# Down projection: two products' activations stored as high and low parts, read back ready-made, and seven weight tiles instead of four

## The chip, the cores and the metric

The kernel runs on one core of one Trainium2 chip, as one program. The metric is the device time of that program in microseconds. A core has five engines that run their own instruction streams and meet only at semaphores: TensorE (PE, matrix products), VectorE (DVE), ScalarE (ACT), GpSimd (POOL) and SyncE (SP, which here issues most DMA transfers). An instruction that waits for a semaphore holds up everything behind it on its own engine; this holds for the DMA issues on SP too.

## The reference, cut to what matters

One encoder layer on 1024 tokens of width 1024: a modulated norm, one input projection, attention and mLSTM heads, an output projection, then the feed-forward part and a final norm. The change lies in the feed-forward part, whose hidden width is 2816:

```python
h = modulate(rms_norm(x, norm_ffn_g[l]), sh2, sc2)
ffn = (jax.nn.silu(h @ w_gate[l]) * (h @ w_up[l])) @ w_down[l]
x = x + g2[:, None, :] * ffn
return rms_norm(x, final_norm_g)
```

All inputs and outputs are float32.

## The kernel before, in words

**High and low parts.** A float32 matrix product is made of three TensorE products of rounded operands (`mm3`, L311 to L314): each operand x is split into a high part (a copy into the type fp32r, made by ACT) and a low part (x minus the high part, made by DVE or POOL), and high·high, high·low and low·high are added up in one PSUM bank. For the activations of the down projection these parts are the tiles `whi` and `wlo` (six buffers each, from the pool `wp`), for its weights `wch` and `wcl`.

**The gate and up stage.** The 2816 hidden columns are 22 tiles of 128; two of them are a pair, p = 0 to 10. For each pair the kernel forms the gate and up products by a seven-product scheme (Strassen's kind, over halves of the width and halves of the tokens), and then, in `act_sums` (L1632), the left operands that the down projection's own seven products need: sums and differences of four blocks of the activation. `store_act` writes them to device memory as the tensors `act_d[p][m]`, 128x512 each, by DMAs on ACT's queue.

**The down projection.** `DOWN` names its seven products in the order in which they run: 11, 21, T2, T3, T1, 22, T4. A product sums over the eleven pairs. One pair of one product, called a step below, is twelve 128x512 matmuls: four output tiles times the three of `mm3`. (T4 runs as two halves of 128x256.) In `down` (L1732) a step first waits for its activation parts and its weight parts, then runs, and then calls three things for what comes later:

- `load_piece`, which asks for the activation of the sixth step ahead. Before, this is a load from `act_d` into one of three tiles `wst` on SP's queue (issued up to two pieces earlier still), then a split by ACT (`whi`) and POOL (`wlo`; on DVE in T4's second half);
- `load_w`, which makes the next weight parts from weight rows that lie in SBUF: ACT copies `wch`, DVE subtracts `wcl`, four buffers each. For T2 DVE first makes two differences (a11 - a21 and `s`), and one more behind `wcl`: four DVE operations for a pair;
- `load_rows`, which issues the pending loads in the list `todo` on SP's queue: the weight rows `wd` of `w_down` (512 KB each, 22 of them) and the tiles `x` of the residual. It goes on while the planner's estimate of the DMA backlog is below 4 us, and issues at least one.

**Names of weight rows.** In the instruction lists `wd` is followed by c (0 or 1: which tile of the pair) and p: `wd10` is c = 1, p = 0, `wd010` is c = 0, p = 10. Product 11 uses rows with c = 0, product 21 rows with c = 1, T2 both. The first five pairs of product 11 take their weights by another way (a 256 KB load, split like an activation), because the weight rows can only be loaded when the pools of the gate and up stage are closed. That happens in `open_down` (L1660), once all stores of activations (`stored`) are done.

**What sets the order.** The kernel is written as Python generators and chains that run against a planner's clock (`Clock`), and the instructions are emitted in the order in which that clock reaches them. A tile asked for from a pool takes over the buffer of the oldest tile of its name; the instruction that writes it waits until the last reader of the old one is done.

Of the kernel before, what the change touches and what calls it, by code (L numbers as in the profile page):

```python
# [11 lines left out]
F32 = mybir.dt.float32  # L12
F32R = mybir.dt.float32r
BF16 = mybir.dt.bfloat16
AF = mybir.ActivationFunctionType
# [5 lines left out]
P = 128  # L21
S = 1024
D = 1024
KT = D // P
HALF = 512
# [18 lines left out]
KB = 5  # L44
AHEAD = 2
NP = NF // 2
# [3 lines left out]
FF = [("b", p) for p in range(NB)] + [("v", 0)] + [("s", (p, i)) for p in range(1, NP - 1) for i in range(2)] + [("v", NP - 1)]  # L50
SET = ["A11", "A12", "S2", "S3", "S1", "A22", "S4"]
DOWN = ["11", "21", "T2", "T3", "T1", "22", "T4"]

# [196 lines left out]
def layer_kernel(ctx, tc, xT, c, w_ada, vecs, cons, rope, w_f, w_fT, w_t0, w_t, w_o, w_gu, w_d, out):  # L250
# [42 lines left out]
    ya_d = [dram.tile([P, S], F32, name=f"ya_d{i}") for i in range(4)]  # L293
    x1_d = [dram.tile([P, S], F32, name=f"x1_d{i}") for i in range(KT)]
    act_d = [{m: dram.tile([P, HALF], F32, name=f"act_d{p}{m}") for m in DOWN} for p in range(NP)]

# [68 lines left out]
    with tc.manual_schedule():  # L365
# [44 lines left out]
        def pair_w(p):  # L410
            order = ("A11", "A12", "S2", "S3", "S4", "S1", "A22") if p else ("S4", "S2", "S3", "S1", "A22")
            return [("set", (p, i, m)) for m in order for i in range(2)]

        def down_w():
            out = []
            for m in DOWN:
                for c in range(2 if m == "T4" else 1):
                    for p in range(NP):
                        a = act_d[p][m]
                        a = a[:, 256 * c:256 * (c + 1)] if m == "T4" else a  # L420
                        n = 2 if m == "T4" else 4
                        out.append((a.rearrange("p (a b) -> p a b", a=n), n, P, c))
                        if m == "11" and p < KB:
                            out.append((w_d[2 * p][:, 0:HALF].rearrange("p (a b) -> p a b", a=4), 4, P))
            return out
# [62 lines left out]
        def load_piece():  # L488

            i = len(pieces)  # L490
            if i == len(specs):
                return
            while len(made) <= min(i + (AHEAD if i + AHEAD >= start["down"] else 0), len(specs) - 1):
                piece(len(made))
            p, there, st = made[i]
            pieces.append(p)
            if isinstance(specs[i][0], str):
                set_piece(p, *specs[i][1])
                return
            split(p, 0.0, lambda: st[0], [P, *specs[i][1:3]], there,  # L500
                  lo=dve if specs[i][3:] == (1,) or i < 9 or start["m", 2] <= i < start["b", 1] else None)
# [1130 lines left out]
        def act_sums(p):  # L1632
            S, T = SG[p], {}
            stored.append(Flag())
            end = stored[-1]
            for m in ("22", "21"):
                ck.chain(0.0, a_ok[p, m], lambda m=m: store_act(p, m, S[m]))

            def new(m, a, b):
                T[m] = fp.tile([P, HALF], F32, tag="tt", name="tt", bufs=4)  # L1640
                dve.tensor_sub(T[m], a, b)

            ck.chain(0.0, a_ok[p, "12"], a_ok[p, "22"], lambda: new("T3", S["22"], S["12"]),
                     lambda: store_act(p, "T3", T["T3"]), a_ok[p, "11"],
                     lambda: dve.tensor_sub(S["12"], S["12"], S["11"]), lambda: store_act(p, "T1", S["12"]),
                     lambda: new("T2", S["22"], S["12"]), lambda: store_act(p, "T2", T["T2"]), a_ok[p, "21"],
                     lambda: new("T4", S["21"], T["T2"]), lambda: store_act(p, "T4", T["T4"]), flag=end)

# [5 lines left out]
        x1_ok = {(k, n): Flag() for k in range(KT) for n in range(NH)}  # L1654
        wseq = [(m, c, p) for m in DOWN for c in range(2 if m == "T4" else 1) for p in range(NP)
                if m != "11" or p >= KB]
# [3 lines left out]
        def open_down():  # L1660
# [16 lines left out]
            load_rows()  # L1677
            for _ in range(4):
                load_w()
# [9 lines left out]
        def load_w():  # L1689
# [32 lines left out]
            def hi():  # L1722
                e[0] = pb.tile([P, HALF], F32R, tag="wch", name="wch", bufs=4)
                act.activation(e[0], src, AF.Copy)

            def lo():
                e[1] = pb.tile([P, HALF], F32R, tag="wcl", name="wcl", bufs=4)
                eng.tensor_sub(e[1], src, e[0].bitcast(F32))
# [3 lines left out]
        def down():  # L1732
            i = start["down"]
            flat = lambda t: t.rearrange("p a b -> p (a b)")
            for m in DOWN:
                for c in range(2 if m == "T4" else 1):
                    w = 256 if m == "T4" else HALF
                    banks = []
                    for p in range(NP):
                        t = pieces[i]  # L1740
# [5 lines left out]
                        for o in range(4):  # L1746
                            if p == 0:
                                yield [slot("acc")]
                                banks.append(psum_tile([P, w], "acc"))
                            mm3(banks[o][0], [x[:, o * P:(o + 1) * P] for x in wt], [flat(x) for x in t[:2]],  # L1750
                                p == 0, p == NP - 1)
                            ck.pe(0.65 * w / HALF)
# [3 lines left out]
                        if opened3.done and not early:  # L1756
                            load_w()
                        if m == "22" and p < 4:
                            load_w()
# [557 lines left out]
```

## Time and profile before

| | us |
|---|---|
| median of 3 runs | 1377.88 |
| lowest and highest run | 1376.33, 1381.36 |
| time of the profiled execution | 1373.45 |
| span of the profiled execution (first to last instruction) | 1371.6 |
| PE busy in the span | 1279.8 (93%) |
| DVE, ACT, POOL busy | 1043.1, 708.9, 697.2 |

All times are microseconds from the span's start. The profiled execution took 1373.45 us, of which 1.85 us lie around its span, and is 4.4 us shorter than the median. The gate and up stage ends and the down projection's first matmul starts at 1130.52; the first 128x256 matmul (T4) starts at 1325.48.

### The profile page before, as it was taken

The numbers are of one execution on the slowest core, as the hardware profiler recorded it, in microseconds if no ns is written. First come the engines' busy times: TensorE is split into PE (matmuls) and PEld (weight loads), VectorE is DVE, ScalarE is ACT, GpSimd is POOL, SyncE is SP. The second block draws the span as 40 slices with busy tenths as digits, with TensorE's granted clock in tenths as the row PEclk, the third lists the DMA queues.
The fourth block names the chain that finished last, engine by engine and source line by source line (L and its number), as shares of the span: only waits on it lengthen the run. The fifth ranks groups of instructions, "written<-read, shape, count | busy, mean of one in ns | idle before, by whom it ended". The sixth has DMA issues, their size and how long they took to land.

```text
span 1371.6 us, 19596 instructions
## 1 busy us (share of the span) xinstructions
PE 1279.8 (93%) x6596; PEld 1074.1 (78%) x6596; DVE 1043.1 (76%) x1541; ACT 708.9 (52%) x1344; POOL 697.2 (51%) x580
## 2 busy tenths in 40 slices
PE   7889888899999979999999999999999999979997
PEld 5777677788778878877778788888888887857887
DVE  6937698975789748768698989877766654998876
ACT  6576366688577755454477522333333234344462
POOL 0353577655558436687605155545454455545542
PEclk9999999999999999999999999999999999989999
DMA  9444433233233146562553344332233159623324
GB/s 360 158 134 142 122 90 96 75 97 109 66 113 99 61 133 195 186 235 100 192 191 116 101 145 151 126 107 101 102 113 116 62 186 349 255 78 107 100 59 157
DMA packets 105044, 188.07 MB, mean 137 GB/s; under 512 B 11632, under 2 KB 33264, under 8 KB 104944
## 3 DMA queue, kind: packets, MB, share of 16 engines
q1 hardware_dynamic: 91552, 164.73, 37.6%
q10 hardware_dynamic: 13392, 22.10, 4.2%
q8 instruction: 52, 0.85, 0.3%
q14 instruction: 48, 0.39, 0.1%
HBM read 139.86 MB, written 43.25 MB: 133 GB/s over the span
## 4 chain that ended last, share of the span: by engine, by line
PE 55%; DVE 20%; issue 8%; ACT 6%; POOL 5%; DMA 4%; SPq 1%; DVEq 0%; ACTq 0%; POOLq 0%
PE acc L314 14%; PE acc L312 14%; PE acc L313 14%; DVE sst L98 3%; DVE y L98 3%; DVE x L98 2%; PE av L1210 2%; DVE PT L98 2%; PE T L1191 2%; PE S L1159 2%; POOL wlo L98 1%; DVE wd L98 1%; DVE s L98 1%; DVE Cs L98 1%; PE ni L1997 1%
## 5 line engine op out<-in xcount | busy, mean ns | idle before, releaser
L98 POOL TENSOR_TENSOR wlo<-wst,whi 128x512 fp32r<-128x512 f32 (+2 forms) x191 | 272.2, 1431 | 293.3 <-ACT whi L98 239.9
L98 ACT ACTIVATE whi<-wst 128x512 fp32r<-128x512 f32 (+2 forms) x223 | 133.1, 605 | 114.2 <-PE acc L314 27.6
L313 PE MATMUL acc<-x,whi 128*128 128x512 f32 x352 | 136.9, 389 | 0.0
L98 POOL TENSOR_SCALAR P<-P,sst 128x1024 f32<-128x1024 f32 x64 | 86.8, 1357 | 87.8 <-DVE sst L98 66.9
L98 POOL TENSOR_TENSOR wlo<-wr,whi 128x512 fp32r<-128x512 f32 x52 | 72.2, 1389 | 71.5 <-ACT whi L98 68.5
L312 PE MATMUL acc<-hh,whi 128*128 128x512 f32 x224 | 97.1, 433 | 7.7 <-ACT xp L98 6.2
L312 PE MATMUL acc<-whi,wch 128*128 128x512 f32 x244 | 96.8, 397 | 5.4 <-ACT wch L98 5.4
L314 PE MATMUL acc<-whi,wcl 128*128 128x512 f32 x244 | 96.8, 397 | 2.9 <-DVE wcl L98 2.8
L313 PE MATMUL acc<-wlo,wch 128*128 128x512 f32 x244 | 96.4, 395 | 0.2 <-POOL wlo L98 0.2
L98 ACT ACTIVATE P<-S,sst,colq 128x1024 f32<-128x1024 f32 x64 | 77.2, 1206 | 35.1 <-DVE sst L98 28.8
L98 DVE TENSOR_TENSOR PT<-T,PT 128x512 fp32r<-128x512 f32 x128 | 83.4, 681 | 9.3 <-ACT PT L98 9.1
L313 PE MATMUL acc<-hl,whi 128*128 128x512 f32 x224 | 90.0, 402 | 0.0
L314 PE MATMUL acc<-hh,wlo 128*128 128x512 f32 x224 | 89.8, 401 | 0.0
L98 ACT ACTIVATE whi<-wr 128x512 fp32r<-128x512 f32 x56 | 35.4, 632 | 100.2 <-DVE wr L98 49.1
L98 ACT ACTIVATE PT<-T 128x512 fp32r<-128x512 f32 x128 | 71.8, 596 | 28.6 <-PE T L1191 27.9
L1191 PE MATMUL T<-ident,P 128*128 128x128 f32 x512 | 72.2, 279 | 15.3 <-DVE PT L98 10.4
L312 PE MATMUL acct<-whi,hh 128*128 128x256 f32 (+1 forms) x256 | 81.6, 319 | 4.9 <-ACT hh L98 3.6
L98 DVE TENSOR_REDUCE sst<-S 128x1 f32<-128x1024 f32 x64 | 77.7, 1214 | 10.4 <-PE S L1159 8.9
L98 POOL TENSOR_TENSOR wlo<-s,whi 128x512 fp32r<-128x512 f32 x40 | 55.1, 1377 | 49.1 <-ACT whi L98 49.1
L1191 PEld LDWEIGHTS T<-ident,P 128*128 128x128 f32 x512 | 59.2, 143 | 25.9 <-issue 9.8
L98 POOL TENSOR_TENSOR ada<-ada,cond 128x512 f32<-128x512 f32 x48 | 68.1, 1419 | 21.9 <-DMA ada<-in_w_ada_dram 21.4
L98 DVE TENSOR_TENSOR wcl<-wd,wch 128x512 fp32r<-128x512 f32 x50 | 51.4, 1041 | 35.7 <-ACT wch L98 35.5
(486 smaller groups left out, 3853.9 us busy)
## 6 DMA issues: line engine op xcount, KB each, us to landing
wr<-in_w_gu_dram SPq DMA_DIRECT2D x66, 256.0 KB, 2.7
ada<-in_w_ada_dram SPq DMA_DIRECT2D x64, 256.0 KB, 3.3
wd<-in_w_d_dram SPq DMA_DIRECT2D x22, 512.0 KB, 6.4
wst<-in_w_gu_dram SPq DMA_DIRECT2D x42, 256.0 KB, 3.0
wst<-act_d SPq DMA_DIRECT2D x33, 256.0 KB, 4.2
ada<-in_w_ada_dram SPq DMA_DIRECT2D x16, 512.0 KB, 7.3
wst<-in_w_o_dram SPq DMA_DIRECT2D x32, 256.0 KB, 3.8
act_d<-sg ACTq DMA_DIRECT2D x29, 256.0 KB, 2.1
```

Of the source, the lines that this page charges most:

```text
L98: return fn(*args, **kw)
L312: nc.tensor.matmul(acc, w[0], x[0], start=first, stop=False)
L313: nc.tensor.matmul(acc, w[0], x[1], start=False, stop=False)
L314: nc.tensor.matmul(acc, w[1], x[0], start=False, stop=last)
L1159: nc.tensor.matmul(sp[:, halves(n)], qs[:, j * P:(j + 1) * P], k2[g][m][:, halves(n)], start=m == 0, stop=m == 1)
L1191: nc.tensor.transpose(tp[:, k], Pt[q][:, (4 * b + k) * P:(4 * b + k + 1) * P], ident)
L1210: nc.tensor.matmul(av, va[:, k, h // 4], PT[it][m][:, k], start=(k, m) == (0, 0), stop=(k, m) == (NJ - 1, 1))
L1997: nc.tensor.matmul(ni, x["q"][:, i * P:(i + 1) * P], H["Cs"][b][:, i4], start=True, stop=True)
```

## The change

Three things are changed.

1. For products 21 and T2 (`PARTS`), `act_sums` no longer stores the activation itself. At the end of a pair's chain it makes the high part on ACT (a new tile `th`, one buffer) and the low part on DVE (in place), and stores both as `part_d[p][m, 0]` and `[m, 1]`, by two DMAs instead of one. In the down projection `load_piece` loads these two straight into `whi` and `wlo`; the split by ACT and POOL goes for those 22 steps.
2. The order of pairs in a product (`turn`) is 0 to 10 for products 11 and 21, as before, and 5 to 10 and then 0 to 4 for the other five.
3. `wch` and `wcl` have seven buffers instead of four, and `open_down` asks for seven weight tiles ahead.

```diff
+PARTS = ("21", "T2")
...
+        def turn(m):
+            return [*range(NP)] if m in ("11", "21") else [*range(KB, NP), *range(KB)]
+
         def down_w():
             out = []
             for m in DOWN:
                 for c in range(2 if m == "T4" else 1):
-                    for p in range(NP):
+                    for p in turn(m):
+                        if m in PARTS:
+                            out.append(("parts", (p, m)))
+                            continue
...
+            if specs[i][0] == "parts":
+                q, m = specs[i][1]
+                for x, tag in enumerate(("whi", "wlo")):
+                    p[x] = lined(tag, [P, 4, P])
+                    arrive = dma(p[x].rearrange("p a b -> p (a b)").bitcast(F32), part_d[q][m, x])
+                ck.chain(arrive, lambda: None, flag=p[2])
+                return
...
-            for m in ("22", "21"):
-                ck.chain(0.0, a_ok[p, m], lambda m=m: store_act(p, m, S[m]))
+            ck.chain(0.0, a_ok[p, "22"], lambda: store_act(p, "22", S["22"]))
...
+            def parts(m, t):
+
+                def hi():
+                    T[m, 0] = fp.tile([P, HALF], F32R, tag="th", name="th", bufs=1)
+                    act.activation(T[m, 0], t(), AF.Copy)
+
+                def lo():
+                    dve.tensor_sub(t().bitcast(F32R), t(), T[m, 0].bitcast(F32))
+
+                def store():
+                    for i, x in enumerate((T[m, 0].bitcast(F32), t())):
+                        f = Flag()
+                        stored.append(f)
+                        ck.chain(dma(part_d[p][m, i], x, nc.scalar), lambda: None, flag=f)
+
+                return hi, lo, store
...
-                     lambda: new("T2", S["22"], S["12"]), lambda: store_act(p, "T2", T["T2"]), a_ok[p, "21"],
-                     lambda: new("T4", S["21"], T["T2"]), lambda: store_act(p, "T4", T["T4"]), flag=end)
+                     lambda: new("T2", S["22"], S["12"]), a_ok[p, "21"],
+                     lambda: new("T4", S["21"], T["T2"]), lambda: store_act(p, "T4", T["T4"]),
+                     *parts("21", lambda: S["21"]), *parts("T2", lambda: T["T2"]), flag=end)
...
-            for _ in range(4):
+            for _ in range(7):
                 load_w()
...
-                e[0] = pb.tile([P, HALF], F32R, tag="wch", name="wch", bufs=4)
+                e[0] = pb.tile([P, HALF], F32R, tag="wch", name="wch", bufs=7)
...
-                    for p in range(NP):
+                    for at, p in enumerate(turn(m)):
```

How the instructions move is shown at two places. The first is SP's queue where the weight rows of product 21 are loaded. Before, these are the rows from the last activation of product 11 (`act_d1011`) on; `act_d021` is product 21's activation of pair 0, and each load into `wst` waits for POOL, which empties that tile.

```order
L317 DMA wst_11393<-act_d1011_184 128x512 [waits DMAHW1_49,Pool_49]
L317 DMA wst_11407<-act_d021_115 128x512 [waits DMAHW2_49,Pool_49]
L317 DMA wd10_11269<-in_w_d_dram 128x1024 [waits DMAHW3_49]
L317 DMA wd11_11270<-in_w_d_dram 128x1024 [waits DMAHW4_49]
L317 DMA wst_11424<-act_d121_122 128x512 [waits DMAHW5_49,Pool_49]
L317 DMA wd12_11271<-in_w_d_dram 128x1024 [waits DMAHW6_49]
L317 DMA wd13_11272<-in_w_d_dram 128x1024 [waits DMAHW7_49]
L317 DMA wd14_11273<-in_w_d_dram 128x1024 [waits DMAHW0_49]
L317 DMA wst_11460<-act_d221_129 128x512 [waits DMAHW1_49,Pool_49]
```

The same place on SP's queue now; `part_d5210` is the high part of product 21's pair 5, `part_d5211` its low part, and so on.

```order
L320 DMA whi_11611<-part_d5210_134 128x512 [waits DMAHW2_49,PE_49,Pool_49]
L320 DMA wlo_11613<-part_d5211_135 128x512 [waits DMAHW3_49]
L320 DMA wd10_11427<-in_w_d_dram 128x1024 [waits DMAHW4_49]
L320 DMA whi_11652<-part_d6210_138 128x512 [waits DMAHW5_49,PE_49]
L320 DMA wlo_11654<-part_d6211_139 128x512 [waits DMAHW6_49]
L320 DMA wd11_11428<-in_w_d_dram 128x1024 [waits DMAHW7_49]
L320 DMA whi_11673<-part_d7210_142 128x512 [waits DMAHW0_49,PE_49]
L320 DMA wlo_11675<-part_d7211_143 128x512 [waits DMAHW1_49]
L320 DMA wd12_11429<-in_w_d_dram 128x1024 [waits DMAHW2_49]
L320 DMA whi_11694<-part_d8210_146 128x512 [waits DMAHW3_49,PE_49]
```

The weight rows of product 21 stood between activations of its own first pairs, two or three at a time; now each of them stands alone behind a load of parts that is five pairs ahead of it (`wd10` behind the parts of pair 5), and that load waits for PE, which reads the old contents of the same `whi` buffer. By the six buffers, the parts of pair 5 of product 21 replace product 11's activation of pair 10, those of pair 6 replace product 21's pair 0, those of pair 7 its pair 1, and so on: in the built program the semaphore value of each such wait is that of the last matmul of that step.

The second place is ACT's queue at the end of the gate and up stage, for the last pair. Before, `act_d10T2`, `act_d1021` and `act_d10T4` are the stores of that pair's T2, 21 and T4.

```order
L317 DMA act_d10T2_186<-tt_11196 128x512 [waits DMAHW5_49,DVE_49]
L317 DMA act_d1021_185<-sg_11020 128x512 [waits DVE_49]
L98 ACTIVATE whi_11218<-wst_11161 128x512 [waits DMAHW1_49,PE_49,Pool_49]
L317 DMA act_d10T4_190<-tt_11212 128x512 [waits DMAHW0_49,DVE_49]
L98 ACTIVATE whi_11231<-wst_11188 128x512 [waits DMAHW2_49,PE_49]
L98 ACTIVATE whi_11254<-wst_11221 128x512 [waits DMAHW6_49,PE_49,Pool_49]
```

The same place on ACT's queue now:

```order
L99 ACTIVATE whi_11340<-wst_11285 128x512 [waits DMAHW5_49,PE_49,Pool_49]
L320 DMA act_d10T4_234<-tt_11335 128x512 [waits DMAHW2_49,DVE_49]
L99 ACTIVATE th_11343<-sg_11144 128x512
L99 ACTIVATE whi_11356<-wst_11312 128x512 [waits DMAHW6_49,PE_49]
L320 DMA part_d10210_154<-th_11343 128x512 [waits DMAHW4_49,Activation_49]
L320 DMA part_d10211_155<-sg_11144 128x512 [waits DVE_49]
L99 ACTIVATE th_11365<-tt_11320 128x512 [waits DMAHW4_49]
L320 DMA part_d10T20_156<-th_11365 128x512 [waits DMAHW7_49,Activation_49]
L320 DMA part_d10T21_157<-tt_11320 128x512 [waits DMAHW0_49,DVE_49]
L99 ACTIVATE whi_11386<-wst_11345 128x512 [waits DMAHW1_49,PE_49,Pool_49]
```

The stores of 21 and T2 moved from ahead of T4's store to behind it. The second `th` takes the one buffer of the first, and so waits, on ACT, until the first high part has been stored; the splits `whi` for product 11 stand behind it. On TensorE the order of the twelve matmuls of each step is unchanged. On POOL the run of `wlo` splits in the down projection has 49 rows instead of 71.

More of the change, by code (lines that the diff above doesn't have):

```diff
@@ L294, in layer_kernel @@
     x1_d = [dram.tile([P, S], F32, name=f"x1_d{i}") for i in range(KT)]
+    part_d = [{(m, i): dram.tile([P, HALF], F32, name=f"part_d{p}{m}{i}") for m in PARTS for i in range(2)}
+              for p in range(NP)]
     act_d = [{m: dram.tile([P, HALF], F32, name=f"act_d{p}{m}") for m in DOWN} for p in range(NP)]
@@ L1654, in layer_kernel @@
         x1_ok = {(k, n): Flag() for k in range(KT) for n in range(NH)}
-        wseq = [(m, c, p) for m in DOWN for c in range(2 if m == "T4" else 1) for p in range(NP)
+        wseq = [(m, c, p) for m in DOWN for c in range(2 if m == "T4" else 1) for p in turn(m)
                 if m != "11" or p >= KB]
@@ L1722, in hi @@
             def hi():
-                e[0] = pb.tile([P, HALF], F32R, tag="wch", name="wch", bufs=4)
+                e[0] = pb.tile([P, HALF], F32R, tag="wch", name="wch", bufs=7)
                 act.activation(e[0], src, AF.Copy)
             def lo():
-                e[1] = pb.tile([P, HALF], F32R, tag="wcl", name="wcl", bufs=4)
+                e[1] = pb.tile([P, HALF], F32R, tag="wcl", name="wcl", bufs=7)
                 eng.tensor_sub(e[1], src, e[0].bitcast(F32))
@@ L1746, in down @@
                         for o in range(4):
-                            if p == 0:
+                            if at == 0:
                                 yield [slot("acc")]
@@ L1750, in down @@
                             mm3(banks[o][0], [x[:, o * P:(o + 1) * P] for x in wt], [flat(x) for x in t[:2]],
-                                p == 0, p == NP - 1)
+                                at == 0, at == NP - 1)
                             ck.pe(0.65 * w / HALF)
@@ L1757, in down @@
                             load_w()
-                        if m == "22" and p < 4:
+                        if m == "22" and at < 4:
                             load_w()
```

## The prediction

> **What bounds the kernel now.** The page's head says that TensorE is busy 93% of the span. I then read the busy times by stretch, to see where the rest is (columns: stretch, its length, busy time of PE, PEld, DVE, ACT and POOL with instruction counts, granted TensorE clock, DMA share, GB/s).
>
> ```profile
> PE 1279.8 (93%) x6596; PEld 1074.1 (78%) x6596; DVE 1043.1 (76%) x1541; ACT 708.9 (52%) x1344; POOL 697.2 (51%) x580
> ...
> 1090.00:1130.00 40.00, 40.00 (x178) 33.15 (x177) 23.50 (x29) 12.60 (x21) 20.09 (x15) 1.00 0.52 172
> 1160.00:1190.00 30.00, 30.00 (x135) 24.82 (x133) 27.55 (x32) 12.92 (x22) 15.75 (x12) 1.00 0.89 342
> 1200.00:1220.00 20.00, 12.90 (x41) 9.52 (x41) 19.90 (x24) 9.36 (x18) 8.90 (x6) 0.74 0.32 93
> 1220.00:1240.00 20.00, 19.06 (x82) 14.80 (x81) 18.93 (x19) 9.30 (x17) 11.52 (x8) 1.00 0.32 83
> ```
>
> In the gate and up stage (first stretch) PE never stops. In product 21 (second) it doesn't either, with DMA at 0.89. It stops in product T2 (third): 7.1 us idle, DVE busy 19.90 of 20, and the clock at 0.74. The waits of PE over the six full-width products (us in total, times, longest) name what ended them:
>
> ```profile
> PE acc L312 <- ACT wch L98: 5.4, 3, 4.7
> PE acc L314 <- DVE wcl L98: 2.8, 2, 2.4
> PE acc L314 <- POOL wlo L98: 0.5, 1, 0.5
> PE acc L313 <- POOL wlo L98: 0.2, 1, 0.2
> ```
>
> So it is T2's weight parts, not its activations, that PE waits for. The timeline of PE gives the sizes (start, duration, idle time before in brackets):
>
> ```profile
> 1130.52 0.39 PE L312 MATMUL acc<-whi 128*128 128x512 f32 x1
> ...
> 1205.59 0.80 PE L312 MATMUL acc<-whi,wch 128*128 128x512 f32 x1 [4.67 <-ACT wch L98]
> ...
> 1209.24 0.80 PE L314 MATMUL acc<-whi,wcl 128*128 128x512 f32 x1 [2.43 <-DVE wcl L98]
> ...
> 1210.26 0.63 PE L313 MATMUL acc<-wlo,wch 128*128 128x512 f32 x1
> 1210.69 0.63 PE L314 MATMUL acc<-whi,wcl 128*128 128x512 f32 x1
> ...
> 1216.09 0.39 PE L313 MATMUL acc<-wlo,wch 128*128 128x512 f32 x1
> 1216.31 0.39 PE L314 MATMUL acc<-whi,wcl 128*128 128x512 f32 x1
> ...
> 1325.48 0.28 PE L312 MATMUL acc<-whi,a 128*128 128x256 f32 x1
> ```
>
> At full clock matmuls start 0.227 us apart, so a step of twelve takes 2.72. The six products are 792 matmuls, 179.5 us at that pitch; from 1130.52 to 1325.48 they took 195.0. Of the 15.4 lost, about 1 lies in product 11 (the two POOL waits and the restart behind them) and 14 around T2. After the wait of 4.67 the pitch is 0.43: half the clock. When it fell and when it came back, by half microseconds (PE busy, clock, DMA share, GB/s):
>
> ```profile
> 1205.00:1205.50 0.50, 0.00 (x0) 0.67 0.00 0
> 1215.00:1215.50 0.50, 0.50 (x3) 0.59 0.68 143
> ```
>
> It fell some 4.3 us after PE had stopped (at 1200.9), and came back some 6 us after the unbroken run from 1209.24 began.
>
> **The change, part by part.** *What it removes.* Why T2's weights are late, from the costliest groups of DVE and POOL between 1188 and 1236 (times, then busy us and mean ns of one):
>
> ```profile
> L98 DVE TENSOR_TENSOR s<-wd,wd 128x512 f32<-128x512 f32 x10 | 12.8, 1280 | 0.0
> L98 DVE TENSOR_TENSOR wd<-wd,s 128x512 f32<-128x512 f32 x11 | 10.7, 983 | 0.0
> L98 DVE TENSOR_TENSOR wd<-wd 128x512 f32<-128x512 f32 x10 | 10.1, 1014 | 0.0
> L98 DVE TENSOR_TENSOR wcl<-s,wch 128x512 fp32r<-128x512 f32 x10 | 9.0, 903 | 2.0 <-ACT wch L98 2.0
> ...
> L98 POOL TENSOR_TENSOR wlo<-wst,whi 128x512 fp32r<-128x512 f32 x17 | 25.1, 1489 | 26.5 <-ACT whi L98 26.5
> ```
>
> Four DVE operations for a pair are 1.28 + 0.98 + 1.01 + 0.90 = 4.2 us, more than a step of 2.72. The change takes the 22 POOL splits and the 22 ACT splits out of 21 and T2, starts T2 with the pairs whose rows come first, and lets DVE run seven tiles ahead. I take the whole 14 us as saved (bounds 8 to 14: the last five pairs of T2 get their first rows only while T2 runs, though needed six steps later).
>
> *Gate and up stage.* For a pair there are two more ACT copies, two more DVE subtractions, two more DMAs on ACT's queue, and ACT waits there until the first `th` is stored (2 to 3 us). I cost it at nothing: in the first stretch above ACT is idle 27 of 40 us and DVE 16, and PE takes its weights from six buffers. If DVE came late to a PSUM bank, PE would show it: bounds 0 to +3.
>
> *The end of that stage.* Here it is on the path, since the weight rows wait for the last store. The chain before: DVE's T4 sum, its store on ACT's queue, the first `wd` on SP's, `wch`, `wcl`, and the first matmul that needs them; behind it the usual landing time of a store (us from issue):
>
> ```profile
> 1133.99 1.67 DVE L98 TENSOR_TENSOR tt<-sg,tt 128x512 f32<-128x512 f32 x1
> ...
> 1135.69 0.33 ACTq L317 DMA_DIRECT2D act_d10T<-tt  x1
> ...
> 1138.92 0.81 SPq L317 DMA_DIRECT2D wd<-in_w_d_dram  x2
> ...
> 1143.45 0.63 ACT L98 ACTIVATE wch<-wd 128x512 fp32r<-128x512 f32 x1 [1.24 <-DMA wd<-in_w_d_dram]
> ...
> 1144.17 0.69 DVE L98 TENSOR_TENSOR wcl<-wd,wch 128x512 fp32r<-128x512 f32 x1 [8.51 <-ACT wch L98]
> ...
> 1144.97 0.39 PE L312 MATMUL acc<-whi,wch 128*128 128x512 f32 x1
> ...
> act_d<-sg ACTq DMA_DIRECT2D x29, 256.0 KB, 2.1
> ```
>
> There is no slack: `wcl` was ready at 1144.86. Now behind T4's store stand on ACT `th` (0.63), a `whi` (0.63), the store of the first `th`, which the second `th` waits for (2.1), that copy (0.63), DVE's subtraction (0.69) and its store: the last store is issued at about 1135.7 + 0.3 + 1.3 + 2.1 + 0.6 + 0.7 = 1140.7 instead of 1135.7. The weight rows, and product 11 from its sixth pair on, come 5 us later. The splits of the fifth pair stand behind the same wait and come late by less. Bounds +3 to +9 (stores of 3 us; rows of the last pairs that now wait for steps 7 and 8).
>
> *Product 21.* This decides. By the order of SP's queue, `wd10`, without which 21 can't begin, stands behind the parts of pair 5, and these wait until the last step of product 11 has read its `whi`. `wd11`, for pair 1, stands behind parts that wait for 21's own first step, and so on: each of the eleven steps begins with a load that was issued only when the step ahead of it had ended. Before, the rows went out well ahead (the first pair of them at 1152.69, some 9 us before product 11 ended), and seven weight tiles don't help, as the rows aren't there. The prices of the link:
>
> ```profile
> 1152.69 1.24 SPq L317 DMA_DIRECT2D wd<-in_w_d_dram  x2
> 1163.14 1.37 SPq L317 DMA_DIRECT2D wd<-in_w_d_dram  x3
> ...
> wd<-in_w_d_dram SPq DMA_DIRECT2D x22, 512.0 KB, 6.4
> ...
> wst<-act_d SPq DMA_DIRECT2D x1, 256.0 KB, 4.2
> ...
> DMA to landing us min/median/max: 3.5/3.8/4.4
> ```
>
> Three issues in 1.37 us are 0.47 apart, so `wd` goes out 0.95 after the parts. How long it takes behind 512 KB of parts on an otherwise empty queue no row shows. The last row is for the three 512 KB loads of `wagain` alone (3.5 at the least); 6.4 is `wd`'s median while the queues are full; 4.2 is a 256 KB load (at 1109.14) behind four others issued within 2.4 us. The last is the nearest case, and I take 4.2 (bounds 3.5 and 6.4). Then come 0.63 for `wch` and some 0.2 (an estimate, from the 0.1 between `wch` and `wcl` and as much at PE and SP) for the meetings: PE is idle 0.95 + 4.2 + 0.63 + 0.2 = 6.0 us a step (bounds 5.3 and 8.2).
>
> The step itself: at full clock its third matmul waits for `wcl` (0.69 behind `wch`), and it lasts 0.75 + 9 x 0.227 + 0.39 = 3.2 us; at half clock 11 x 0.427 + 0.63 = 5.3. A gap of 6.0 is longer than the 4.3 after which the clock fell, and 5.3 of work is shorter than the 6 after which it came back, so most steps run at half clock. Cycle: 9.2 to 11.3, I take 11.0. Against 2.72 that is 8.3 more, eleven times: +91 us (bounds 11 x (5.3 + 3.2 - 2.72) = +64 and 11 x (8.2 + 5.3 - 2.72) = +119).
>
> The Trainium skill, "TensorE: Matmul & The Clock Gate", Part 1, has the clock judged by free-running windows of about 3.4 us: half after a window without work, full after one window of work. This trace's fall after 4.3 us agrees; its return after 6 us is at the far end of what such windows allow. By the page a step of 5.3 us would often contain a whole busy window and end at full clock, which gives back at most some 0.8 us a step, by an estimate from the page: +82 instead of +91.
>
> *T2 and after.* All rows that T2's first six pairs need have landed in 21, and DVE has had ten microseconds a step for its four operations. Its first steps may run at half clock: +2. The later products keep their code; 0.
>
> *Sum.* +5 + 91 + 2 - 14 = +84 on the profiled execution's 1373.45 us: 1457. The three runs have their median 4.4 us above that execution, so I put the forecast at 1460.
>
> **The rivals.** *A lead of one step.* If the wait ahead of `wd` ended a step sooner than I read it, the idle time would be 6.0 - 2.72 = 3.3 us a step, too short for the clock to fall: 11 x 3.6 = +40, less 14, plus 5, so 1409. For it: PE's queue runs ahead in loading weights. Against it: the load overwrites `whi`, which the last matmul of the step reads.
>
> *The rows are in time (the other side).* If the part loads did not hold up the rows behind them, by three steps or more (8.2 us, above the 6.0 of the link), 21 would run through, only the opening would cost 5, and T2's 14 would be saved: 1377.9 + 5 - 14 = 1369. For it: SP's waits cost PE nothing in 21 before, with DMA at 0.89. Against it: those were waits for POOL with the rows ahead of them.
>
> *Only the first row is late.* If later rows caught up while PE waits, the price would be one link, 6 us: 1377.9 + 5 + 6 - 14 = 1375. Against it: one row stands behind each load of parts, eleven times; none can pass.
>
> **How the numbers follow.** The chain of eleven late rows: 0.88. A lead of one step: 0.05. Rows in time: 0.04. One late row: 0.03. The range, from 1433 (opening 3, 64 a product, less 12) to 1486 (nearer the middle than the upper bound of 119, which needs the full queue's landing time on an idle one), leaves some of both ends out with the rivals. A measurement of this kernel can tell about 0.5%, 7 us, from no change: slower 0.93, same 0.03, faster 0.04.
>
> **What would show it.** In the changed kernel's trace: eleven gaps of PE of about 6 us in product 21, ended by ACT's `wch` with `wd` in flight; issues on SP in threes, each just behind the end of a step; the clock near 0.5 to 0.7 in 21; 21 longer than 100 us; no long wait in T2; the first `wd` issued near 1144. I am wrong if `wd` lands in much under 4 us, if the clock holds, or if SP issues rows while a step runs.

## The result, and the profile after

The changed kernel takes 1468.45 us (median of four runs, 1466.09 to 1474.66); the kernel before took 1377.57 beside it (four runs). The ratio is 1.066, with a 95% interval of 1.062 to 1.069. The profiled execution of the changed kernel took 1466.09 us, with a span of 1464.3: 92.7 more than the span before.

The page's head, and behind it the busy times by stretch, with the columns of the table of stretches before:

```profile
PE 1305.3 (89%) x6596; PEld 1087.6 (74%) x6596; DVE 1035.1 (71%) x1563; ACT 708.0 (48%) x1344; POOL 671.3 (46%) x558
```

```profile
1090.00:1130.00 40.00, 40.00 (x179) 33.11 (x178) 23.52 (x31) 13.65 (x23) 20.18 (x15) 1.00 0.55 183
1130.00:1170.00 40.00, 35.13 (x136) 26.25 (x134) 12.52 (x17) 12.08 (x20) 15.22 (x12) 0.91 0.78 266
...
1200.00:1220.00 20.00, 9.68 (x24) 6.96 (x24) 1.39 (x2) 1.26 (x2) 0.00 (x0) 0.67 0.24 81
...
1300.00:1340.00 40.00, 40.00 (x178) 33.13 (x177) 31.42 (x44) 16.62 (x29) 15.16 (x10) 1.00 0.62 205
```

The gate and up stage (first row) still keeps PE busy without a gap, and T2 (last row) now does so too. In product 21 (third row) everything is idle at once: PE half of the time, DVE and ACT nearly always, POOL always, DMA at 0.24. Where no resource is busy, time goes into a chain of latencies. The waits of PE from 1130 to 1430 (us in total, times, longest) say which engine hands over last:

```profile
PE acc L315 <- ACT wch L99: 71.3, 13, 6.9
PE acc L315 <- ACT whi L99: 2.9, 1, 2.9
...
```

One link of that chain, by the timelines of PE, SP and ACT (start, duration, idle time before):

```profile
1200.93 0.79 PE L315 MATMUL acc<-whi,wch 128*128 128x512 f32 x1 [5.43 <-ACT wch L99]
...
1205.69 0.40 PE L317 MATMUL acc<-whi,wcl 128*128 128x512 f32 x1
1212.54 0.79 PE L315 MATMUL acc<-whi,wch 128*128 128x512 f32 x1 [6.45 <-ACT wch L99]
```

```profile
1206.12 0.32 SPq L320 DMA_DIRECT2D whi<-part_d  x1
1206.48 0.43 SPq L320 DMA_DIRECT2D wlo<-part_d  x1
1206.96 0.43 SPq L320 DMA_DIRECT2D wd<-in_w_d_dram  x1
```

```profile
1211.86 0.63 ACT L99 ACTIVATE wch<-wd 128x512 fp32r<-128x512 f32 x1 [10.98 <-DMA wd<-in_w_d_dram]
```

The step's last matmul ends at 1206.09. SP, which had stood waiting for it, issues the parts 0.03 us later and the weight row 0.87 after that end; 4.90 us later the row is there and ACT starts; 0.68 later the next step starts. There are eleven such gaps, ten of them 5.4 to 6.5 us long and the first 6.95. From 1177.17 to 1291.82 there are ten cycles, 11.47 us each.

The lengths of the products show where the 92.7 us are (first matmul of a product to that of the next; product 21 of the changed kernel from the end of product 11's last step, at 1170.2):

| us | 11 | 21 | T2 | T3 | first matmul to T4 |
|---|---|---|---|---|---|
| before | 31.4 | 29.9 | 42.8 | 31.0 | 195.0 |
| after | 39.5 | 126.9 | 30.3 | 29.9 | 286.5 |

Product 21 costs 97.0 more, the opening 8.1 more; T2 gives 12.5 back and T3 1.1.

### The profile page after: what moved, and what is told of

Its sections match the earlier page's. It is cut to its first block, busy times and chain, and to the rows that moved or that the text cites. A ratio compares the mean times of both kernels' runs of the same rounds, so it can differ in the third digit from the quotient of the medians.

```text
span 1464.3 us, 19615 instructions
## 1 busy us (share of the span) xinstructions
PE 1305.3 (89%) x6596; PEld 1087.6 (74%) x6596; DVE 1035.1 (71%) x1563; ACT 708.0 (48%) x1344; POOL 671.3 (46%) x558
## 4 chain that ended last, share of the span: by engine, by line
PE 55%; DVE 17%; DMA 9%; issue 8%; ACT 5%; POOL 4%; SPq 2%; ACTq 0%; DVEq 0%; POOLq 0%
PE acc L315 15%; PE acc L317 14%; PE acc L316 14%; DMA wd<-in_w_d_dram 4%; DVE sst L99 3%; DVE x L99 2%; DVE y L99 2%; DVE PT L99 2%; PE av L1226 2%; PE T L1207 2%; SPq L320 2%; PE S L1175 1%; POOL wlo L99 1%; DVE Cs L99 1%; PE acct L317 1%
## 5 line engine op out<-in xcount | busy, mean ns | idle before, releaser
L99 POOL TENSOR_TENSOR wlo<-wst,whi 128x512 fp32r<-128x512 f32 (+2 forms) x169 | 241.3, 1434 | 423.4 <-ACT whi L99 404.3
L99 ACT ACTIVATE whi<-wst 128x512 fp32r<-128x512 f32 (+2 forms) x201 | 120.0, 603 | 122.4 <-POOL wlo L99 29.1
L315 PE MATMUL acc<-whi,wch 128*128 128x512 f32 x244 | 107.0, 438 | 71.3 <-ACT wch L99 71.3
L99 DVE TENSOR_TENSOR wcl<-wd,wch 128x512 fp32r<-128x512 f32 x50 | 47.6, 956 | 127.5 <-ACT wch L99 127.3
L315 PEld LDWEIGHTS acc<-whi,wch 128*128 128x128 f32 x244 | 51.3, 210 | 87.8 <-ACT wch L99 78.2
L317 PE MATMUL acc<-whi,wcl 128*128 128x512 f32 x244 | 103.7, 425 | 0.7 <-DVE wcl L99 0.7
L316 PE MATMUL acc<-wlo,wch 128*128 128x512 f32 x244 | 103.7, 425 | 0.0
L99 ACT ACTIVATE wch<-wd 128x512 fp32r<-128x512 f32 x50 | 31.2, 624 | 124.3 <-DMA wd<-in_w_d_dram 114.1
L1207 PE MATMUL T<-ident,P 128*128 128x128 f32 x512 | 70.7, 275 | 16.5 <-DVE PT L99 11.4
```

Source lines behind the costliest of these rows:

```text
L99: return fn(*args, **kw)
L315: nc.tensor.matmul(acc, w[0], x[0], start=first, stop=False)
L316: nc.tensor.matmul(acc, w[0], x[1], start=False, stop=False)
L317: nc.tensor.matmul(acc, w[1], x[0], start=False, stop=last)
L1207: nc.tensor.transpose(tp[:, k], Pt[q][:, (4 * b + k) * P:(4 * b + k + 1) * P], ident)
```

## The experiments

**The theories.** A: each step of 21 waits for a weight row that stands in SP's queue behind loads of parts, which wait for the end of the step ahead; its place in the queue is the cause. B: the doubled bytes of the activations are the cause, wherever the rows stand. Besides, it was open how much the half clock costs, what the opening's loss hangs on, and which part of the change saves T2's time. Each kernel was timed beside the kernel before on the same chip; that kernel's median there is given. Single profiled executions begin the down projection anywhere from 1127.9 to 1137.5 us, also where two kernels differ only behind that point, so stages are compared by their lengths and kernels by their medians. The lengths of stages are those of one execution each; where it lay far from its kernel's median, the text says so.

### 1. The rows of 21 one step further ahead

```diff
-        def load_rows():
+        def load_rows(most=99):
...
-            while todo and (ck.dma_t - ck.now < 4.0 or n == 0):
+            while todo and (ck.dma_t - ck.now < 4.0 or n == 0) and n < most:
...
+                        if m == "21":
+                            load_rows(1)
                         load_piece()
...
-                        load_rows()
+                        if m != "21":
+                            load_rows()
```

> Theory A (each weight row of product 21 is issued on SP only when the step before has ended): here the same rows are issued one step earlier, one row a step from the second on. The first row still costs 6.9 us, then two steps pass for one link of 6.4 idle plus 3.2 of work, a cycle near 4.8 instead of 11.5, and the clock is mostly full: product 21 about 60 us instead of 127, total 1402 (1392 to 1415). Rival B (the doubled bytes of the activations make DMA the limit in 21, whatever the order): unchanged within 10 us, 1460 to 1475.

Measured: 1414.05 us beside 1376.21, 1.028 (1.026 to 1.030). Three of PE's waits by its timeline:

```profile
1193.61 0.50 PE L315 MATMUL acc<-whi,wch 128*128 128x512 f32 x1 [2.84 <-ACT wch L99]
1204.84 0.52 PE L315 MATMUL acc<-whi,wch 128*128 128x512 f32 x1 [3.60 <-ACT wch L99]
1215.97 0.80 PE L315 MATMUL acc<-whi,wch 128*128 128x512 f32 x1 [3.69 <-ACT wch L99]
```

The stretch around the second of them, with the clock in the third column from the end:

```profile
1200.00:1210.00 10.00, 6.39 (x21) 4.57 (x20) 2.59 (x4) 1.26 (x2) 0.00 (x0) 0.83 0.54 200
```

With the same bytes, one place in the queue takes some 52 us off (1.066 to 1.028 of 1376), so B falls. PE now waits at every second step only, and two steps go through one turn of the loop of 11.2 us (1193.61 to 1204.84 to 1215.97). A had 9.6 for it, and so 1402: the gaps of about 3 us, which it took to be too short for the clock to fall, still bring it to a mean of 0.83.

### 2. PE kept busy for part of the gap

```diff
+                            for _ in range(16):
+                                nc.tensor.matmul(spare, a[0][:, 0:P], a[1], start=True, stop=True)
```

> Each step of product 21 is followed by sixteen more matmuls into a PSUM bank that nobody reads (3.6 us at full clock), so that TensorE works for a part of each gap; the loads wait for the same matmuls as before. If theory A has the sizes right, idle plus these matmuls is the same 6.4 us a step, the clock stays full and a step of work lasts 3.2 instead of about 5: 11 x 1.9 = 20 us less, 1448 (1442 to 1456). If the half clock is not what lengthens the steps (rival C): 1468, or more by what the added matmuls cost.

Measured: 1463.76 us beside 1376.21, 1.065 (1.062 to 1.069). A miss: nothing like the 20 us came back. The profiled execution took 1475.86 us, the longest of the four (the others 1461.45 to 1465.08). A gap that is left in it, and the clock around it by half microseconds:

```profile
1195.18 2.68 PE L1791 MATMUL acc<-wcl,wch 128*128 128x512 f32 x11
1200.02 0.50 PE L315 MATMUL acc<-whi,wch 128*128 128x512 f32 x1 [2.16 <-ACT wch L99]
```

```profile
1201.00:1201.50 0.50, 0.50 (x3) 0.41 (x3) 0.00 (x0) 0.00 (x0) 0.00 (x0) 1.00 0.00 0
1201.50:1202.00 0.50, 0.50 (x3) 0.36 (x3) 0.00 (x0) 0.00 (x0) 0.00 (x0) 0.61 0.00 0
...
1204.50:1205.00 0.50, 0.50 (x3) 0.40 (x2) 0.00 (x0) 0.00 (x0) 0.00 (x0) 0.50 0.00 0
1205.00:1205.50 0.50, 0.50 (x4) 0.41 (x3) 0.00 (x0) 0.00 (x0) 0.00 (x0) 0.98 0.00 0
```

PE is idle for 2.16 us, from 1197.86 to 1200.02. The clock falls 1.6 us after work has resumed, at 1201.6, and returns at 1205.0, 3.4 us later. So the experiment did not take the half clock away and doesn't price it; number 8 repeats it with the gap nearly filled.

### 3. The rows early

```diff
-            while todo and (ck.dma_t - ck.now < 4.0 or n == 0):
+            while todo and (ck.dma_t - ck.now < 8.0 or n == 0):
```

> The planner's limit for weight rows is 8 us of modelled backlog instead of 4; the row of pair k of product 21 then stands ahead of the parts of pair k + 1 instead of behind those of k + 5. Theory A: no wait over 2 us in product 21, T2's 14 us stay saved, the opening still costs 8: 1372 (1366 to 1382). Rival B (bytes): DMA share 1.0 through products 11 and 21, with waits for rows and parts: over 1395.

Measured: 1370.38 us beside 1376.21, 0.995 (0.994 to 0.997). SP's queue where product 21's rows are issued:

```profile
1161.72 0.43 SPq L320 DMA_DIRECT2D wd<-in_w_d_dram  x1
1162.82 0.32 SPq L320 DMA_DIRECT2D whi<-part_d  x1
1163.41 0.32 SPq L320 DMA_DIRECT2D wlo<-part_d  x1
1164.02 0.33 SPq L320 DMA_DIRECT2D wd<-in_w_d_dram  x1
```

The first row of 21 goes out at 1161.72, some 9 us before its first step, instead of behind the end of product 11; the parts of six pairs stood ahead of it in the changed kernel, those of one pair do here. Product 21 takes 31.1 us and T2 29.9, with all the doubled loads in place. So the chain came from position; by themselves the doubled bytes cost product 21 about 1 us. What is left of the loss is the opening, 37.8 us instead of 31.4.

### 4. As 3, the last pair's 21 and T2 stored whole

```diff
+                tail += parts(m, t) if by_parts(m, p) else [lambda m=m, t=t: store_act(p, m, t())]
```

Here `by_parts` holds for the first ten pairs.

> As the run before, and the last pair (p = 10) is stored and split in the old way, so that ACT doesn't wait for a store at the end of the gate and up stage. If the 8 us that product 11 lost come from that wait, they go: 1364 (1359 to 1370). If they come from the added DMAs or from the pools closing late for another reason: no different from the run before.

Measured: 1370.00 us beside 1376.21, 0.995 (0.994 to 0.997): as without that edit. The first row goes out 11.3 us after the stage's first matmul instead of 16.2, and the fourth and fifth steps of product 11 take 3.2 and 5.0 us instead of 5.5 and 7.4. But the tenth and eleventh now take 5.3 each, and product 11 39.7 in all:

```profile
1170.73 0.50 PE L321 MATMUL acc<-whi,wch 128*128 128x512 f32 x1 [2.38 <-ACT whi L105]
1172.08 0.50 PE L322 MATMUL acc<-wlo,wch 128*128 128x512 f32 x1 [0.84 <-POOL wlo L105]
```

The wait at the start was real; taken away, another comes behind it in this execution, which at 1374.74 us was the longest of the eight.

### 5. The order of pairs and the seven tiles alone

```diff
+def by_parts(m, p):
+    return False
```

No parts at all; the stores of 21 and T2 stay behind T4's.

> Left of the change: the turned order of pairs in T2 and its successors and the seven weight tiles; every activation is stored and loaded whole again, once, as before. It asks what T2's 14 us hung on. Theory D (order and lead of DVE): T2's first steps waited in the kernel before because DVE came to the quadrant sums late and in the order of pairs whose rows came last; then this kernel alone saves 8 to 14 us: T2 at 30 to 34 us, total 1361 to 1368. Theory E (the splits on ACT and POOL held T2 up): T2 stays at 38 to 43 us and the total at 1372 to 1378. In both, product 21 is 30 us with no gap, since each row of weights is issued ahead of what waits for a buffer.

Measured: 1372.18 us beside 1374.57, 0.997 (0.995 to 0.998). T2 takes 36.5 us, between the two theories: a good 6 of the 12.5 come from the order and the tiles. DVE stays the last to hand over (waits of PE, 1130 to 1430):

```profile
PE acc L323 <- DVE wcl L105: 4.3, 3, 2.2
PE acc L321 <- ACT wch L105: 1.8, 2, 1.0
PE acc L322 <- POOL wlo L105: 1.2, 1, 1.2
```

Unexpected: product 11 takes 34.4 us here, though there is no `th` to wait for. SP's queue:

```profile
1139.66 1.56 SPq L326 DMA_DIRECT2D wst<-act_d  x2
1142.12 0.81 SPq L326 DMA_DIRECT2D wd<-in_w_d_dram  x2
```

The stage begins at 1130.93, so the first row goes out after 11.2 us instead of 8.4. That led to number 9.

### 6. Parts for T2 alone

```diff
+def by_parts(m, p):
+    return m == "T2"
...
-                        if m in PARTS:
+                        if by_parts(m, p):
```

> Parts for the third product alone; the second's activations are stored whole and split on load as before. The loads in product 21 are then the old ones (256 KB a pair), but T2's parts are still asked for in the steps of 21 and behind them the rows of weights. If the bytes and the place in SP's queue are what made the chain in 21, rows stay ahead while 21's whole activations are loaded, and a late row can come only where T2's parts begin, in its last steps: 21 at 30 to 33 us, T2 at 30 to 33, opening 0 to 5 longer: total 1364 to 1371. If the chain needs only a load of parts ahead of a row, anywhere, there are gaps of about 6 us from the place where T2's parts begin (each costing 6 to 8 us): total over 1400.

Measured: 1367.81 us beside 1374.57, 0.9935 (0.991 to 0.996). It is the fastest by its median of all that were run. Product 11 takes 33.4, 21 33.2 and T2 29.9 us: with the order and the tiles in place, taking the splits out of T2 brings it to its floor of 29.9 (132 matmuls at 0.227). Whether it would without the turned order, no run here asks. The lengths are those of the longest of the six executions, 1371.01 us.

### 7. As 3, with four tiles

```diff
-            for _ in range(7):
+            for _ in range(4):
                 load_w()
...
-                e[0] = pb.tile([P, HALF], F32R, tag="wch", name="wch", bufs=7)
+                e[0] = pb.tile([P, HALF], F32R, tag="wch", name="wch", bufs=4)
```

> As the kernel with the rows early (rows issued eight, not four, microseconds ahead of the planner's clock), but with four split weight tiles of each kind instead of seven. If the lead of three more tiles is what lets DVE (four operations and 4.2 us a pair) keep up in T2, T2 gets its stall back in part: 33 to 40 us, total 1374 to 1381. If the order of pairs and the splits taken out suffice, T2 stays at 30 us and the total at 1366 to 1374.

Measured: 1369.26 us beside 1374.57, 0.996 (0.994 to 0.998). Products 11, 21 and T2 take 37.7, 31.3 and 29.9 us, in number 3 37.8, 31.1 and 29.9 (here in the shortest of twelve executions, 1365.06 us): with parts and early rows, three more weight tiles are worth nothing.

### 8. The gap nearly filled

```diff
+                            for _ in range(24):
+                                nc.tensor.matmul(spare, a[0][:, 0:P], a[1], start=True, stop=True)
```

> The changed kernel with 24 more matmuls of 128x128 by 128x512 behind each step of product 21, into a bank that nothing reads (they use no weight row); 16 left gaps of 2 to 3 us, and the clock still fell once in each. 24 at 0.227 take 5.4 us of the 6.4 us gap, so PE should be idle 1 us or less a step. If the half clock within the steps is a price of the idle time, the clock now stays at 1.0, a step takes about 3.2 us, the cycle 9.6 instead of 11.5: total 1443 to 1452. If the gaps alone set the cycle (landing time under whatever clock), it stays at 1460 to 1470.

Measured: 1457.92 us beside 1374.57, 1.059 (1.056 to 1.062). The first and the last of the nine cycles by PE's timeline, and a stretch of them:

```profile
1192.24 0.50 PE L315 MATMUL acc<-whi,wch 128*128 128x512 f32 x1 [0.65 <-ACT wch L99]
...
1278.69 0.50 PE L315 MATMUL acc<-whi,wch 128*128 128x512 f32 x1 [1.16 <-ACT wch L99]
```

```profile
1220.00:1270.00 50.00, 45.03 (x185) 33.72 (x185) 15.02 (x23) 6.30 (x10) 0.00 (x0) 1.00 0.31 105
```

The clock holds at 1.00 through nine cycles with gaps of 0.6 to 1.2 us, and a cycle is 86.45 / 9 = 9.61 us, as expected for a full clock. So the half clock is 11.47 - 9.61 = 1.9 us a step, 20 of the 97 us; the other 76 are the link itself (11 x (9.61 - 2.72)). The total came out 6 us above the range that was given: the first link still ran at half clock (12.6 us) and the last 24 matmuls (5.4 us) stand behind 21's last step with nothing to cover.

### 9. As 5, the stores in the old order

```diff
-            ck.chain(0.0, a_ok[p, "22"], lambda: store_act(p, "22", S["22"]))
+            for m in ("22", "21"):
+                ck.chain(0.0, a_ok[p, m], lambda m=m: store_act(p, m, S[m]))
```

T2's store also goes back to its place ahead of T4's.

> As the kernel with the turned order and seven tiles alone, but the gate and up stage stores in the order of the kernel before: the second product's activation as soon as it is there, the third's ahead of the fourth sum's. In the kernel without parts, 21's and T2's stores stood behind T4's, and the first weight row of the down projection was issued 11.2 us after that stage's first matmul instead of 8.4, though no split and no extra copy was there. Theory F: that delay, and the 3.0 us that product 11 lost in it, come from the order of the last pair's stores; then the first row is back at 8.4 to 9 us, product 11 at 31 to 32 us, and the total 2 to 4 us below that kernel: 0.994 to 0.996 of before, 1366 to 1370. Theory G: the order of the stores is innocent and the delay comes from the rest of the plan; then the row stays at 11 and the total at 0.997, 1370 to 1374. T2 is 36 us in both.

Measured: 1380.12 us beside 1376.61, 1.004 (1.002 to 1.005). As to the opening theory F holds: the first row goes out 8.4 us after the stage's first matmul, and product 11 takes 31.3. The total went the other way: 21 takes 38.3 us and T2 38.8, so that of T2's 12.5 us only 4.0 are left. PE's timeline:

```profile
1189.60 0.51 PE L321 MATMUL acc<-whi,wch 128*128 128x512 f32 x1 [2.29 <-ACT whi L105]
1190.95 0.79 PE L322 MATMUL acc<-wlo,wch 128*128 128x512 f32 x1 [0.85 <-POOL wlo L105]
1219.43 0.79 PE L322 MATMUL acc<-wlo,wch 128*128 128x512 f32 x1 [6.33 <-POOL wlo L105]
```

The first two waits lie in 21; number 10 shows where they come from. The third lies in T2. The split that it waits for took POOL 10.79 us, from 1208.59 on, where the median of the eleven splits around it is 1.29; DVE was busy without a pause from 1208 to 1218.3, and the split ended 1.1 us later. That DVE's run is the cause was not tested.

### 10. Parts for T2 in ten pairs, the last pair as before

```diff
+    return m == "T2" and p < NP - 1
```

The stores are those of number 9 where no parts are made.

> A version that should beat both: parts for the third product alone and only for ten pairs, the last pair of the gate and up stage stored as in the kernel before, in the old order; turned order, seven tiles. By the runs so far: T2 30 us (13 saved), 21 31 to 33 us (1 to 3 lost to DVE's late split of a row), product 11 31 to 33 us (0 to 2 lost): 9 to 12 saved, 1363 to 1366, 0.991 to 0.993 of before. If the last pair's order of stores has nothing to do with the opening, it is as the kernel with T2's parts for all pairs, 0.9935, or worse by the POOL split of the last pair in T2's step 6.

Measured: 1370.73 us beside 1376.61, 0.996 (0.994 to 0.997); above what was expected. Product 11 is mended (32.1) and T2 is at 29.9, but 21 takes 38.2, as in number 9. ACT's queue, and the longest of PE's waits in 21, show why:

```profile
1181.65 0.63 ACT L105 ACTIVATE wch<-s 128x512 fp32r<-128x512 f32 x1 [5.10 <-DVE s L105]
...
1186.60 0.63 ACT L105 ACTIVATE wch<-s 128x512 fp32r<-128x512 f32 x1 [3.28 <-DVE s L105]
1188.67 0.63 ACT L105 ACTIVATE wch<-s 128x512 fp32r<-128x512 f32 x1 [1.44 <-DVE s L105]
1189.21 1.13 ACT L105 ACTIVATE whi<-wst 128x512 fp32r<-128x512 f32 x2
```

```profile
1189.88 0.80 PE L321 MATMUL acc<-whi,wch 128*128 128x512 f32 x1 [2.28 <-ACT whi L105]
```

The early weights of T2 (`wch` out of `s`) stand on ACT ahead of the splits that product 21 needs next, and wait for DVE: first 5.1 us, while DVE still adds up product 11's output and makes low parts for 21, then 3.3 and 1.4, while it makes T2's differences. The first of these costs PE little; behind the other two it stops for 2.28 us.

### 11. As 10, with the rows early

```diff
-            while todo and (ck.dma_t - ck.now < 4.0 or n == 0):
+            while todo and (ck.dma_t - ck.now < 8.0 or n == 0):
```

> The same with the rows issued eight, not four, microseconds ahead of the planner's clock. If an early row only helps, the 1 to 3 us that 21 lost go as well: 21 at 30 to 31 us, total 1361 to 1365. If early rows take the place of the activations' loads in the opening (the fourth and fifth steps of product 11 took 5.5 and 7.4 us where rows came early, 3.6 and 4.9 where they did not), product 11 gets longer by 3 to 5 us and the total is 1366 to 1370.

Measured: 1372.75 us beside 1376.61, 0.996 (0.995 to 0.998). Product 21 falls to 32.4, product 11 rises to 35.5 (sixth and seventh steps 5.3 and 5.4): as the second theory had it for the opening, with a total above both ranges. In the profile 21 wins 5.8 us and the opening loses 3.5. But this execution, at 1364.73, was the shortest of the twelve, 8 us below their median; what the others lose, and where, no trace here shows.

### 12. Both products in parts for ten pairs, rows early from the sixth pair

```diff
+    return m in PARTS and p < NP - 1
...
-                        load_rows()
+                        load_rows(8.0 if m != "11" or p >= 5 else 4.0)
```

The last pair is stored as in the kernel before; the limit of number 3 holds from the sixth step of product 11 on.

> The change mended at both places: parts for 21 and T2 for ten pairs; the last pair of the gate and up stage stored and split as in the kernel before, in the old order; rows issued eight microseconds ahead of the planner's clock from the sixth pair of product 11 on, four ahead of it until then. Since 21 has parts, its splits no longer stand on ACT behind T2's early weights, which cost 8 us in the version with parts for T2 alone. By the runs so far: product 11 31 to 33 us, 21 30 to 32, T2 30: 10 to 13 saved, 1363 to 1367, 0.990 to 0.993 of before. If rows ahead cost the opening as much from the sixth pair on as from the first (product 11 at 35 us or more), or the last pair's old split is late in 21's last step, it is 0.995 or above.

Measured: 1372.19 us beside 1375.78, 0.9975 (0.996 to 0.9995): above the range; 0.995 or more was expected where product 11 takes 35 us or more. In the profile 21 and T2 are both at 29.9, and from the stage's first matmul to T4 it takes 185.6 us, the least of all kernels; product 11 takes 36.0. ACT's queue ahead of its eleventh step:

```profile
1159.62 0.63 ACT L105 ACTIVATE wch<-wd 128x512 fp32r<-128x512 f32 x1 [4.50 <-DMA wd<-in_w_d_dram]
1160.35 0.63 ACT L105 ACTIVATE whi<-wst 128x512 fp32r<-128x512 f32 x1
```

And PE, which waits for that split:

```profile
1161.04 0.50 PE L321 MATMUL acc<-whi,wch 128*128 128x512 f32 x1 [2.23 <-ACT whi L105]
```

A split that was ready to go stands behind a weight copy whose row has not landed. The profiled execution, at 1363.4, was the fastest of twelve (up to 1377.22); what the slower ones lose, and where, no trace here shows, and it stays open.

## Why the prediction was right

The forecast was 1460 us for 1468.45 measured, by the chain that it named. No large errors cancel in the sum: by the two profiles the opening cost 3.1 us more than forecast, product 21 6.0 more, and T2 with what follows gave back 1.6 more (13.6 for 14 less 2).

**The main chain held.** Eleven gaps ended by ACT's `wch` with a row in flight, SP's issues in threes just behind a step's end, the clock at 0.59 to 0.67, no long wait in T2: as listed. That it is the row's place in the queue, and not the doubled bytes by themselves, is shown by numbers 1 and 3.

**The link.** The prediction had an idle time of 6.0 us, with 4.2 for the landing, and a cycle of 11.0. Measured: 6.3 in the mean of the ten gaps from 1190.06 on, and 11.47. The landing is the term that was short; over the ten rows behind the first:

```profile
DMA to landing us min/median/max: 3.8/4.7/4.9
```

How much of it is owed to the 512 KB of parts issued just ahead of the row, no run separates; the three loads of 512 KB alone, in the prediction, took 3.5 at the least. The work of a step, 11.47 - 6.3 = 5.2, was put at 5.3 for half clock and counted as 5.0 in the cycle of 11.0. So 21 cost 97 instead of 91.

**The clock.** The prediction's estimate from the Trainium skill, "TensorE: Matmul & The Clock Gate", Part 1, was 82 for product 21. The windows of that page agree with the times of the changes here, read by half microseconds (the clock falls at 1198.7, is back at 1205.5, falls at 1209.0: multiples of 3.4 us):

```profile
1198.50:1199.00 0.50, 0.00 (x0) 0.74 0.97 389
...
1205.50:1206.00 0.50, 0.50 (x3) 0.93 0.00 0
...
1208.50:1209.00 0.50, 0.00 (x0) 0.98 1.05 365
```

But the return comes in the last 0.6 us of a step that ends at 1206.1, so hardly anything is given back. The estimate had up to 0.8 us back in every step; of the ten steps from 1177.17 on only three were that short (4.5 us instead of 5.3). The prediction itself took 4.3 us as the gap after which the clock falls. That is too long, as number 2 shows with 2.16 us; at gaps of 6 us it changed nothing.

**The opening** was put at +5 and cost +8.1. Two things were off. The wait of the second `th` was taken at the usual 2.1 us of a store; ACT's queue has 4.19:

```profile
1141.58 0.63 ACT L99 ACTIVATE th<-tt 128x512 fp32r<-128x512 f32 x1 [4.19 <-DMA part_d<-th]
```

And SP was not free when the last store was done. Three activation loads stood ahead of the rows; they waited for POOL, POOL for ACT, ACT for that store:

```profile
1138.84 8.12 SPq L320 DMA_DIRECT2D wst<-act_d  x3
1147.18 0.81 SPq L320 DMA_DIRECT2D wd<-in_w_d_dram  x2
```

The first row went out at 1147.18; "near 1144" was forecast. That is 16.5 us after the stage's first matmul instead of 8.4, the same 8.1 that product 11 lost. The prediction had the splits behind the wait, but not the SP queue behind the splits. Some 3 us of the loss have nothing to do with `th`: they come with the stores' new order (34.4 us in number 5, 31.3 in number 9).

**T2** gave back 12.5 (and T3 1.1), for 14 forecast within 8 to 14. The prediction named three causes together. The order and the tiles alone give 6.3 of it in number 5 and 4.0 in number 9; with the splits taken out as well it is all there (numbers 6 and 7); and the three more tiles are worth nothing where parts are made (number 7). What the splits alone would give was not run.

**The rivals' prices.** Rows in time was priced at 1369, 9 us below the kernel before; number 3, which makes it so, came out 5.8 below the kernel beside it. A lead of one step was priced at 1409, 31 above; number 1 came out 38 above. That this is near is luck: in its profile product 21 costs 39 us more than before, where the price had 40, but the price had a gap of 3.3 us in every step at full clock, and the run has one of 2.8 to 3.7 in every second step and half clock for part of the time.

## What to carry to other kernels

Before counting what a change saves on an engine, write down the order of the DMA queue that it lengthens: a load that waits for a buffer holds up every load behind it, and one row per waiting load turns a prefetch into a chain, eleven times 6 us here, with every engine idle and DMA at 0.24. Doubling the bytes cost product 21 about 1 us where the rows stood ahead; putting the rows behind them cost 97. Where a transfer must overwrite a buffer, issue what the next step needs ahead of it, and look on the other in-order queues too (here ACT's `wch` ahead of `whi`) for the next thing that waits in front of something ready.

## What the hardware showed that had not been expected

The clock falls after gaps much shorter than the 4.3 us seen before. In number 2 a gap of 2.16 us brought half clock for 3.4 us, beginning 1.6 us after PE had started again; gaps of 0.6 to 1.2 us (number 8) did not. If a verdict is made every 3.4 us over the 3.4 us ahead of it, PE had been idle for 1.8 of the 3.4 that end at 1201.6. This reading can be put to the traces before and after and those of numbers 1, 2 and 8, around products 21 and T2. In each of them all changes of the clock stand on one grid of 3.41 us. All 27 falls end a stretch of that grid in which PE was busy for 47% or less; of the stretches that end with the clock still full, all but one (43%) have PE busy for 50% or more. The 27 returns end stretches with 83% or more. The Trainium skill, "TensorE: Matmul & The Clock Gate", Part 1, asks for a whole idle window; number 2 shows the fall with half of one.

A 256 KB store can take twice its usual time just where its end is waited for: `part_d<-th` landed after 4.7 us, where the last two stores of the same kernel took 2.0 (median us from issue to landing):

```profile
part_d<-th ACTq DMA_DIRECT2D x1, 256.0 KB, 4.7
...
part_d10T<-th ACTq DMA_DIRECT2D x1, 256.0 KB, 2.0
```
